# A hybrid two-layer decoder: mask building and two norms moved between engines, layer 1's rows kept in attention's order, and a planner with other costs

## The chip, the cores and the metric

One core of one Trainium2 chip runs the whole program: 1,024 tokens of width 1,024 through two layers, everything in float32. The engines are TensorE (PE; its weight loads are listed as PEld), VectorE (DVE), ScalarE (ACT), GpSimd (POOL) and SyncE (SP), which issues all DMAs. The metric is the device time of one execution in microseconds (us). The kernel before takes 2319.9 us, the median of three runs from 2319.55 to 2323.67.

## The reference

```python
for l in range(DEPTH):                       # DEPTH = 2
    h = rmsnorm(x, norm_mix_pre[l])
    if l % 2 == 0:
        proj = h @ w_in_even[e]              # 1024 -> 3072
        qa, fa, ia, ga, ub, vb = jnp.split(proj, splits, axis=-1)
        oa = hgrn2_mix(qa, fa, ia, ga, lb_all[l], a_norm[e])
        ob = chunk_gmlp_mix(gelu(ub), gelu(vb), b_ln_g[e], b_ln_b[e], b_ws[e], b_bias[e])
        mix = jnp.concatenate([oa, ob], axis=-1) @ w_out_even[e]
    else:
        mix = dilated_attention_mix(h, w_in_odd[o], positions) @ w_out_odd[o]
    x = x + rmsnorm(mix, norm_mix_post[l])
    h = rmsnorm(x, norm_ffn_pre[l])
    y = jnp.square(jax.nn.relu(h @ w_ff1[l])) @ w_ff2[l]      # 1024 -> 4096 -> 1024
    x = x + rmsnorm(y, norm_ffn_post[l])
```

`chunk_gmlp_mix` takes the layernorm of v over 512 channels, `(v - mu) * rstd * ln_g + ln_b`, and multiplies it in chunks of 128 positions by a causal 128x128 matrix per group of 128 channels, adds a bias per position and multiplies by u. `hgrn2_mix` ends in `rmsnorm(o, a_norm)` per head of 128 channels. The attention has three dilated branches, (128, 1), (512, 4) and (2048, 16), merged by their denominators: a key at distance d counts once, twice or three times, as it lies in one, two or three of them, so one additive mask with -inf, 0, ln 2 and ln 3 holds all three.

## The kernel before

Each float32 operand of a large product is split into a high part (ACT, a copy with rounding) and a low part (DVE or POOL, a subtraction), and each product is three matmuls (high x high, high x low, low x high). Six matmuls of 512 columns, listed as "x6", are one product of two 128-row blocks. `HT` and `WP` are the two large SBUF buffers of split activations and split weights; `b` stands for every other SBUF tile. The PSUM banks are `mm`, `tr`, `pa` and `pb`.

The program is first recorded, operation by operation, by the class `Plan` (`add`, line 257), and then put in order by `run` (line 344), which walks a planned time: at each step it takes an engine's ready operation, books it for its `cost` (line 297), and emits it. What it emits per engine is a list that the engine works off in order, each instruction waiting on semaphores for its inputs and for the release of its buffers. So an operation that has to wait holds up all behind it on its engine, and a cost in the planner changes the order and not the work. Large products are taken in the order of the program among those that are ready; the conversions are fitted in where the planner has an engine idle. A DVE operation that reads two SBUF tensors (`o["pair"]`, line 261) is booked longer while POOL is planned busy (line 459). In the profile nearly all instructions carry line 422, where `emit` issues them.

Stages, in order of time: constants (`consts0`, line 766, prepares the gMLP's transposed causal matrices `wsT` and its bias); layer 0's input projection with the HGRN and gMLP heads (`layer0_mix`, `gmlp_norm` 949, `gmlp_mix` 963, `onorm` 975), about 8 to 330 us; layer 0's output projection, then `ff1` and `ff2` (line 1572) to about 1068 us; attention, 1092 to about 1580; layer 1's output projection (it reads the attention's output back by `reload_oT`, line 1351), `ff1`, and `ff2` from about 2005 us to the end.

`ff2` runs three stages of eight blocks of hidden channels, each block eight products of six matmuls that go to eight PSUM banks, and at a stage's end DVE (and ACT) empty the banks into `y1` and `y2` (lines 1676 to 1685): `b<-tr,b`, `b<-pa,b` and the like in the rows. The first product of the next stage that goes to a bank waits for that. After them come the last products and, row tile by row tile, `post_part` and `post_end` (line 1761), which add the residual and store. Layers 0 and 1 run the same `ff2`; only in layer 0 it also builds the attention's mask: `attn_mask` (line 1093) makes a quarter of a 128x1024 table at each call, in one 128x1024 tile `x` (one buffer for all four calls), and stores it to DRAM (`maskd`).

```python
            if l == 0 and 3 <= m <= 6:                      # line 1687, m counts the blocks
                self.attn_mask(prep, 256 * (m - 3))
```

Each call is 4 iota and 15 further instructions on POOL and 2 on DVE (the two `bitwise_and`), which alternate on the same tile.

Attention works on the rows of a tile of 128 tokens in the order r, r+4, r+8, ... (four residues of 32). In the kernel before, `reload_oT` puts the columns of layer 1's activations back in token order while it splits them, with a strided source and target.

## Time and profile before

| what | us |
|---|---|
| median of three runs | 2319.9 |
| profiled execution | 2320.68 |
| its span, first to last instruction | 2318.9 |
| PE busy | 2259.9 (97% of the span) |
| DVE busy | 1616.1 (70%) |
| ACT busy | 1114.1 (48%) |
| POOL busy | 1097.3 (47%) |
| mean granted TensorE clock | 0.995 of full speed |

A row of the timeline reads: start, duration, engine, line, operation, output<-inputs, shape, count, and in brackets how long the engine was idle just before and who released it. "878.99 2.92 PE ... tr<-WP,HT ... x6 [7.30 <-DVE b L422]" is a product of six matmuls that began at 878.99 us and took 2.92, after PE had waited 7.30 us for a DVE instruction. Rows of the grouped view give count, busy time, mean ns of one, and the idle time before them. Rows of the windows view give start:end, length, and each engine's busy time in it.

### The profile page before, as it was taken

How to read it: one execution, taken by the hardware profiler on the slowest of the kernel's cores; microseconds unless marked ns; L12 is line 12 of the kernel's file. 1: busy time of each engine (PE TensorE's matmuls, PEld its weight loads, DVE VectorE, ACT ScalarE, POOL GpSimd, SP SyncE). 2: the span in 40 equal slices, each digit the busy share in tenths (PEclk: the TensorE clock that was granted, in tenths of full speed). 3: DMA queues.
4: the chain of work that ended last, by engine and by line, in shares of the span. 5: the costliest groups of instructions: out<-in, count | busy, mean ns of one | idle time of the engine just before them, and what ended most of it. 6: DMA issues, size and time to landing. Idle time of an engine off the chain costs nothing.

```text
span 2318.9 us, 32947 instructions
## 1 busy us (share of the span) xinstructions
PE 2259.9 (97%) x11314; PEld 1929.9 (83%) x11314; DVE 1616.1 (70%) x3106; ACT 1114.1 (48%) x2403; POOL 1097.3 (47%) x1184
## 2 busy tenths in 40 slices
PE   8999999999999998999999999998999999999998
PEld 7888778888888787887999999996788888888887
DVE  7688975665555955848888887877765555787746
ACT  6444444442222432435777777787452222433333
POOL 2121453355555889415555555543345555645204
PEclk9999999999999999999999999999999999999999
DMA  5110123334443957754311111114334443877654
GB/s 173 55 35 22 37 82 97 112 111 153 151 150 132 327 203 239 250 206 157 103 46 46 47 46 44 53 43 155 113 132 150 150 151 138 290 277 267 224 176 160
DMA packets 214768, 319.10 MB, mean 138 GB/s; under 512 B 14132, under 2 KB 99144, under 8 KB 214600
## 3 DMA queue, kind: packets, MB, share of 16 engines
q1 hardware_dynamic: 214600, 317.00, 40.5%
q8 instruction: 89, 1.46, 0.3%
q14 instruction: 79, 0.65, 0.1%
HBM read 226.24 MB, written 90.70 MB: 137 GB/s over the span
## 4 chain that ended last, share of the span: by engine, by line
PE 75%; DVE 12%; ACT 4%; POOL 3%; DMA 3%; issue 2%; SPq 0%; DVEq 0%; ACTq 0%; POOLq 0%
PE mm L422 34%; PE pa L422 20%; PE pb L422 13%; PE tr L422 9%; DVE b L422 9%; POOL b L422 3%; ACT b L422 3%; DVE WP L422 2%; DVE HT L422 1%; DMA b<-in_w_ff_dram 1%; DMA b<-in_w_in_odd_dram 1%; DMA b<-oTd 1%; DMA b<-hc 1%; ACT HT L422 0%; ACT WP L422 0%
## 5 line engine op out<-in xcount | busy, mean ns | idle before, releaser
L422 POOL TENSOR_TENSOR b<-b,b 128x512 f32<-128x512 f32 (+4 forms) x500 | 576.4, 1169 | 668.3 <-ACT b L422 324.5
L422 PE MATMUL mm<-WP,HT 128*128 128x512 f32 (+2 forms) x3744 | 822.5, 362 | 3.3 <-DVE HT L422 1.2
L422 PEld LDWEIGHTS mm<-WP,HT 128*128 128x128 f32 x3744 | 655.3, 190 | 82.1 <-DVE HT L422 2.3
L422 ACT ACTIVATE b<-b 128x512 f32<-128x512 f32 (+6 forms) x653 | 327.1, 513 | 369.8 <-POOL b L422 190.0
L422 POOL TENSOR_TENSOR b<-b 128x512 f32<-128x512 f32 (+4 forms) x368 | 331.8, 907 | 352.0 <-DVE b L422 246.0
L422 ACT ACTIVATE WP<-b 128x1024 fp32r<-128x1024 f32 (+2 forms) x248 | 194.3, 792 | 340.2 <-PE pb L422 190.5
L422 DVE TENSOR_TENSOR WP<-b,WP 128x1024 fp32r<-128x1024 f32 (+1 forms) x164 | 225.8, 1385 | 127.9 <-ACT WP L422 127.5
L422 DVE TENSOR_TENSOR b<-b,b 128x1024 fp32r<-128x1024 f32 (+6 forms) x382 | 239.3, 642 | 76.5 <-ACT b L422 58.7
L422 ACT ACTIVATE b<-mm 128x512 f32<-128x512 f32 (+3 forms) x346 | 152.6, 454 | 265.8 <-PE mm L422 246.2
L422 DVE TENSOR_TENSOR HT<-b,HT 128x1024 fp32r<-128x1024 f32 (+3 forms) x131 | 217.9, 1671 | 23.2 <-ACT HT L422 23.0
L422 PE MATMUL tr<-b,b 128*128 128x128 f32 x1074 | 171.1, 278 | 30.2 <-DVE b L422 24.2
L422 PE MATMUL pa<-WP,HT 128*128 128x512 f32 x768 | 193.8, 390 | 0.0
L422 DVE TENSOR_TENSOR b<-tr,b 64x128 fp32r<-64x128 f32 (+5 forms) x404 | 162.7, 407 | 32.8 <-ACT b L422 25.4
L422 PE MATMUL tr<-WP,HT 128*128 128x512 f32 x672 | 171.6, 392 | 7.6 <-DVE b L422 7.3
L422 ACT ACTIVATE HT<-b 128x1024 fp32r<-128x1024 f32 (+4 forms) x147 | 142.6, 973 | 73.8 <-PE mm L422 30.3
L422 PEld LDWEIGHTS tr<-b,b 128*128 128x128 f32 x1074 | 128.9, 147 | 54.1 <-DVE b L422 27.7
L422 PE MATMUL mm<-HT,b 128*128 128x512 f32 x720 | 173.7, 390 | 0.0
L422 PE MATMUL pa<-WP,b 128*128 128x512 f32 x720 | 173.6, 389 | 0.0
L422 DVE TENSOR_TENSOR b<-pa,b 128x512 f32<-128x512 f32 x110 | 75.4, 689 | 135.7 <-PE pa L422 135.6
L422 PEld LDWEIGHTS pa<-WP,HT 128*128 128x128 f32 x768 | 144.2, 188 | 29.9
L422 PEld LDWEIGHTS pa<-WP,b 128*128 128x128 f32 x720 | 134.9, 188 | 27.9
L422 PEld LDWEIGHTS mm<-HT,b 128*128 128x128 f32 x720 | 134.8, 188 | 27.8
(63 smaller groups left out, 3041.1 us busy)
## 6 DMA issues: line engine op xcount, KB each, us to landing
b<-in_w_ff_dram SPq DMA_DIRECT2D x172, 512.0 KB, 4.9
hc<-b SPq DMA_DIRECT2D x224, 256.0 KB, 2.1
b<-hc SPq DMA_DIRECT2D x112, 512.0 KB, 5.6
b<-in_w_in_odd_dram SPq DMA_DIRECT2D x64, 192.0 KB, 2.9
x<-b SPq DMA_DIRECT2D x24, 512.0 KB, 2.7
b<-x SPq DMA_DIRECT2D x24, 512.0 KB, 3.4
b<-in_w_in_even_dram SPq DMA_DIRECT2D x32, 256.0 KB, 2.8
wd<-b SPq DMA_DIRECT2D x16, 512.0 KB, 3.5
```

The source lines that it names most:

```text
L422: return getattr(self.real[eng], meth)(*[x.real() if isinstance(x, View) else x for x in a], **{k: x.real() if isinstance(x, View) else x ...
```

## The change

Five things change.

1. The planner's costs. A function `shares` says which DVE operations are booked longer beside POOL; POOL's costs rise (a 128x512 tensor_tensor from 147 + 2.15 x 512 to 150 + 2.4 x 512 ns); the longer booking itself gets another form.
2. The gMLP's layernorm no longer multiplies by `ln_g` and adds `ln_b` on POOL. The gain is applied after the causal product, as a column per channel group, by a DVE scalar_tensor_tensor of 128x128; the bias goes through the causal matrix once, in the constants (a product of ones with `wsT`, 2 float32 matmuls of 512 columns, and 8 scalar_tensor_tensors).
3. `onorm`: a DVE and a POOL tensor_tensor of 128x512 become four DVE scalar_tensor_tensors of 128x128.
4. `attn_mask`: all but the iota goes from POOL to DVE, and the calls stand at blocks 14, 16, 18 and 20 in place of 3 to 6.
5. Layer 1's rows stay in attention's order: `reload_oT` splits contiguously, its low part always on DVE; the residual rows of layer 1 are loaded, and the output rows stored, in four DMAs of 32 rows each.

```diff
-        o["pair"] = any(sum(isinstance(x, View) and x.buf.n not in self.inpsum and x.shape[-1] > 1
-                            for x in list(a)[1:] + [kw.get("in0"), kw.get("in1")]) > 1 for _, _, a, kw in calls)
+        o["pair"] = any(self.shares(*c) for c in calls)
...
-        return 147 + (2.15 if meth == "tensor_tensor" else 3.3 if meth == "tensor_scalar" else 1.2) * n
+        if meth == "memset":
+            return 62 + 0.83 * n
+        return 150 + (2.4 if meth == "tensor_tensor" else 4.0 if meth == "tensor_scalar" else 1.2) * n
+
+    def shares(self, eng, meth, a, kw):
+        views = [x for x in list(a) + [kw.get("in0"), kw.get("in1")] if isinstance(x, View) and x.shape[-1] > 0]
+        if any(x.buf.n in self.inpsum for x in views) or meth.startswith("dma"):
+            return False
+        out = kw["out"] if "out" in kw else a[0]
+        n = sum(x.shape[-1] > 1 or meth != "tensor_scalar" for x in views if x is not out)
+        return n > 1 or n == 1 and math.prod(out.shape[1:]) > 1
...
-                    end += min(max(free.get("POOL", 0.0) - at, 0.0), max(o["cost"], 700.0))
+                    busy = max(free.get("POOL", 0.0) - at, 0.0)
+                    if busy and now["POOL"]:
+                        busy += o["cost"]
+                    end += min(busy, max(0.85 * o["cost"], 700.0))
...
+                tr = self.tr_bank()
+                with nc.group():
+                    nc.tensor.matmul(tr, self.ones.bitcast(F32), wt.rearrange("p g t -> p (g t)"), start=True, stop=True)
+                for g in range(4):
+                    gs = slice(g * P, (g + 1) * P)
+                    nc.vector.scalar_tensor_tensor(bias[:, gs], tr[:, gs], lnb[:, g:g + 1], bias[:, gs], op0=OP.mult, op1=OP.add)
...
-        nc.gpsimd.tensor_tensor(vn, vn, self.lng, op=OP.mult)
-        nc.gpsimd.tensor_tensor(vn, vn, self.lnb, op=OP.add)
...
-        for i in range(2):
...
-            nc.vector.tensor_tensor(ob[t // 4][i][:, :, t % 4 * P:(t % 4 + 1) * P], part, bias, op=OP.add)
+        for g in range(4):
+            gs = slice(g * P, (g + 1) * P)
+            nc.vector.scalar_tensor_tensor(ob[t // 4][g // 2][:, g % 2, t % 4 * P:(t % 4 + 1) * P], tr[:, gs], self.lng[:, g:g + 1],
+                                           self.bias[t % 2][:, gs], op0=OP.mult, op1=OP.add)
...
-        nc.vector.tensor_tensor(ov, ov, r[:, :, None].to_broadcast([P, 4, P]), op=OP.mult)
-        nc.gpsimd.tensor_tensor(o, o, self.anr, op=OP.mult)
+        for h in range(4):
+            hs = slice(h * P, (h + 1) * P)
+            nc.vector.scalar_tensor_tensor(o[:, hs], o[:, hs], r[:, h:h + 1], self.anr[:, hs], op0=OP.mult, op1=OP.mult)
...
-            G.tensor_copy(u, d)
-            G.tensor_scalar(M, u, 128.0, None, op0=OP.is_le)
+            V.tensor_copy(u, d)
+            V.tensor_scalar(M, u, 128.0, None, op0=OP.is_le)
...
-        src = raw.rearrange("p k (r u) -> p k u r", r=4)
-        hi, lo = (self.HT[:, x, k0:k1, ts].rearrange("p k (u r) -> p k u r", r=4) for x in range(2))
-        nc.scalar.activation(hi, src, AF.Copy)
-        (nc.gpsimd if t < LAG["rel"] else nc.vector).tensor_tensor(lo, src, hi.bitcast(F32), op=OP.subtract)
+        hi, lo = (self.HT[:, x, k0:k1, ts] for x in range(2))
+        nc.scalar.activation(hi, raw, AF.Copy)
+        nc.vector.tensor_tensor(lo, raw, hi.bitcast(F32), op=OP.subtract)
+
+    def rows_of(self, x, t, cs, spread):
+        if not spread:
+            return [(slice(0, P), x[t * P:(t + 1) * P, cs])]
+        return [(slice(32 * r, 32 * r + 32), x[t * P + r:(t + 1) * P:4, cs]) for r in range(4)]
...
-            if l == 0 and 3 <= m <= 6:
-                self.attn_mask(prep, 256 * (m - 3))
+            if l == 0 and m in (14, 16, 18, 20):
+                self.attn_mask(prep, 128 * (m - 14))
...
-        nc.sync.dma_start(x, xin[rows, :])
+        for p, src in self.rows_of(xin, t, slice(0, D), xin is self.x2):
+            nc.sync.dma_start(x[p], src)
...
-                nc.sync.dma_start(xout[rows, d], x[:, d])
+                for p, dst in self.rows_of(xout, t, d, xout is self.out[0]):
+                    nc.sync.dma_start(dst, x[p, d])
```

How the instructions move. First DVE at the end of the first stage of layer 0's `ff2`. `b_6037` is the mask's tile before, `b_6054` after; `b<-tr` and `b<-pa` empty the banks. Before:

```order
L422 TENSOR_SCALAR b_6037<-b_6037 128x256
L422 TENSOR_TENSOR WP<-b_5958,WP 128x1024
L422 TENSOR_TENSOR WP<-b_6063,WP 128x1024
L422 TENSOR_SCALAR b_6037<-b_6037 128x256
L422 TENSOR_TENSOR b_6137<-tr,b_6137 128x512
L422 TENSOR_TENSOR HT<-b_6038,HT 128x2x512
L422 TENSOR_TENSOR b_6205<-tr,b_6205 128x512
L422 TENSOR_TENSOR HT<-b_5939,HT 128x2x512
L422 TENSOR_TENSOR b_5911<-pa,b_5911 128x512 x2
```

and after:

```order
L432 TENSOR_SCALAR b_6054<-b_6054 128x256
L432 TENSOR_TENSOR b_6054<-b_6054 128x256
L432 TENSOR_TENSOR WP<-b_6082,WP 128x1024
L432 TENSOR_TENSOR HT<-b_6105,HT 128x2x512
L432 TENSOR_TENSOR WP<-b_5963,WP 128x1024
L432 TENSOR_TENSOR b_6164<-tr,b_6164 128x512
L432 TENSOR_TENSOR HT<-b_5982,HT 128x2x512
L432 TENSOR_TENSOR b_6143<-tr,b_6143 128x512
L432 CAST b_6054<-b_6054 128x256
L432 TENSOR_SCALAR b_6054<-b_6054 128x256 x3
L432 TENSOR_TENSOR b_6054<-b_6054 128x256
L432 TENSOR_TENSOR b_5935<-pa,b_5935 128x512
```

Before, a mask instruction whose input comes from POOL stands directly ahead of the first emptying of a `tr` bank. After, three masks (54 instructions) are complete ahead of it, and the fourth begins between the `tr` and the `pa` banks, with a CAST whose input is POOL's iota.

Second PE at the end of layer 0, where the first transposes of layer 1's activations (`tr<-b_86`, 128x128) come between the last products of `ff2`. Before:

```order
L422 MATMUL tr<-WP,HT 128x512 x6
L422 MATMUL pa<-WP,HT 128x512 x3
L422 MATMUL tr<-b_86,b_6086 128x128 x4
L422 MATMUL pa<-WP,HT 128x512 x3
L422 MATMUL mm<-b_86,b_6086 128x128 x4
L422 MATMUL pb<-WP,HT 128x512 x6
```

and after:

```order
L432 MATMUL tr<-WP,HT 128x512 x6
L432 MATMUL pa<-WP,HT 128x512 x6
L432 MATMUL pb<-WP,HT 128x512 x6
L432 MATMUL tr<-b_86,b_6104 128x128 x4
L432 MATMUL pa<-WP,HT 128x512 x3
L432 MATMUL mm<-b_86,b_6104 128x128 x4
L432 MATMUL pa<-WP,HT 128x512 x3
```

The transposes stand one and a half products later. Third PE in layer 0's output projection, between two row tiles. Before:

```order
L422 MATMUL mm<-b_625,HT 128x512 x6
L422 MATMUL mm<-b_2727,HT 128x512 x6
L422 MATMUL mm<-WP,HT 128x512 x9
L422 MATMUL tr<-b_86,b_2611 128x128 x8
L422 MATMUL mm<-WP,HT 128x512 x27
```

and after:

```order
L432 MATMUL mm<-b_668,HT 128x512 x6
L432 MATMUL mm<-b_3001,HT 128x512 x6
L432 MATMUL mm<-WP,HT 128x512 x9
L432 MATMUL tr<-b_86,b_2358 128x128 x4
L432 MATMUL mm<-WP,HT 128x512 x6
L432 MATMUL tr<-b_86,b_2358 128x128 x4
L432 MATMUL mm<-WP,HT 128x512 x21
```

The eight transposes of a row tile are cut in two halves with one product between them.

## Rows read from the trace of the kernel before

**Rows 1.** The page's busy times, and from the view of waits who PE waited for (total us, times, longest).

```profile
PE 2259.9 (97%) x11314; PEld 1929.9 (83%) x11314; DVE 1616.1 (70%) x3106; ACT 1114.1 (48%) x2403; POOL 1097.3 (47%) x1184
...
PE tr L422 <- DVE b L422: 31.5, 20, 8.2
PE pa L422 <- DVE b L422: 6.5, 10, 1.9
PE tr L422 <- POOL b L422: 5.6, 6, 3.0
```

**Rows 2.** PE's timeline: the end of layer 0's `ff1` and the first stage of its `ff2` (to 878.99), where its last products begin (1054.62), and the same two places of `ff2` in layer 1 (2005.54 and 2266.78).

```profile
778.66 4.61 PE L422 MATMUL pa<-HT,b 128*128 128x512 f32 x12 [1.85 <-DVE b L422]
783.11 1.53 PE L422 MATMUL mm<-WP,HT 128*128 128x512 f32 x6
...
878.99 2.92 PE L422 MATMUL tr<-WP,HT 128*128 128x512 f32 x6 [7.30 <-DVE b L422]
...
1054.62 1.52 PE L422 MATMUL tr<-WP,HT 128*128 128x512 f32 x6
1055.98 1.52 PE L422 MATMUL pa<-WP,HT 128*128 128x512 f32 x6
...
2005.54 1.52 PE L422 MATMUL mm<-WP,HT 128*128 128x512 f32 x6
...
2266.78 1.52 PE L422 MATMUL tr<-WP,HT 128*128 128x512 f32 x6
```

**Rows 3.** Timeline of DVE and, in the second row, of POOL: two places in layer 0's `ff2` where a mask instruction of DVE stands.

```profile
775.54 2.47 DVE L422 TENSOR_SCALAR b<-b 128x256 int32<-128x256 int32 x1
775.27 2.59 POOL L422 TENSOR_TENSOR b<-b,b 128x1024 f32<-128x1024 f32 x1 [1.87 <-DMA b<-in_w_ff_dram]
...
866.75 0.29 DVE L422 TENSOR_SCALAR b<-b 128x256 int32<-128x256 int32 x1 [12.31 <-POOL b L422]
...
878.04 0.29 DVE L422 TENSOR_SCALAR b<-b 128x256 int32<-128x256 int32 x1 [6.32 <-POOL b L422]
878.25 0.68 DVE L422 TENSOR_TENSOR b<-tr,b 128x512 f32<-128x512 f32 x1
```

**Rows 4.** Windows: the first stage of `ff2` in layer 0, the 16.5 us ahead of layer 1's, and layer 1's first stage. Columns: start:end, length, busy us of PE, PEld, DVE, ACT, POOL with counts, granted clock, DMA share, GB/s.

```profile
783.10:870.10 87.00, 87.00 (x385) 72.05 (x384) 62.61 (x38) 33.99 (x36) 80.26 (x53) 1.00 0.70 246
...
1989.00:2005.50 16.50, 16.50 (x74) 13.69 (x73) 12.23 (x12) 8.25 (x11) 5.82 (x3) 1.00 0.85 295
2005.50:2092.50 87.00, 87.00 (x385) 71.84 (x385) 75.66 (x42) 36.87 (x40) 50.28 (x18) 1.00 0.84 296
```

**Rows 5.** Groups by form on DVE: the mask's integer tensor_scalars in 783 to 957 us (count, busy us, mean ns, idle before), and all tensor_tensors of 128x256 of SBUF tiles in the program.

```profile
L422 DVE TENSOR_SCALAR b<-b 128x256 int32<-128x256 int32 x7 | 2.0, 292 | 45.5 <-POOL b L422 45.5
...
L422 DVE TENSOR_TENSOR b<-b,b 128x256 f32<-128x256 f32 x64 | 31.4, 490 | 1.8 <-PE pa L422 1.5
```

**Rows 6.** The heads of layer 0, 230 to 330 us: PE's wait for POOL, and groups by form on POOL and DVE (the last row are scalar_tensor_tensors of 128x128).

```profile
PE tr L422 <- POOL b L422: 4.9, 5, 3.0
...
L422 POOL TENSOR_TENSOR b<-b,b 128x512 f32<-128x512 f32 x33 | 45.2, 1375 | 71.7 <-DVE b L422 67.2 <-ACT WP L422 2.7 <-PE tr L422 1.3
...
L422 DVE TENSOR_TENSOR b<-tr,b 128x256 f32<-128x256 f32 x16 | 6.0, 413 | 0.0
L422 DVE TENSOR_TENSOR b<-b,b 128x512 f32<-128x512 f32 x8 | 5.4, 679 | 0.0
...
L422 DVE SCALAR_TENSOR_TENSOR b<-b,b,tr 128x128 f32<-128x128 f32 x3 | 1.0, 344 | 0.1
```

**Rows 7.** PE's timeline at the transposes in layer 0's output projection (the first and the last of three such rows) and at the first transposes of layer 1's activations.

```profile
398.78 0.66 PE L422 MATMUL tr<-b,b 128*128 128x128 f32 x4 [0.75 <-DVE b L422]
...
424.30 0.66 PE L422 MATMUL tr<-b,b 128*128 128x128 f32 x4 [0.75 <-DVE b L422]
...
1065.63 0.66 PE L422 MATMUL tr<-b,b 128*128 128x128 f32 x4 [3.37 <-DVE b L422]
```

**Rows 8.** The end of attention: a window of it, then groups by form of the whole program: the splits of `reload_oT` (`HT<-b,HT` 128x512) beside contiguous splits of the same size.

```profile
1564.00:1582.00 18.00, 13.32 (x66) 8.73 (x65) 17.37 (x49) 17.19 (x34) 11.45 (x18) 1.00 0.39 128
...
L422 DVE TENSOR_TENSOR HT<-b,HT 128x512 fp32r<-128x512 f32 x13 | 17.0, 1308 | 4.9 <-ACT HT L422 4.7
L422 DVE TENSOR_TENSOR b<-b,b 128x512 fp32r<-128x512 f32 x42 | 29.8, 709 | 2.6 <-ACT b L422 2.4
```

**Rows 9.** The end of the program on SP's queue (a load, then six stores of half a row tile) and on DVE, and two lines of the list of DMA issues (KB each, median us from issue to landing).

```profile
2297.05 0.33 SPq L422 DMA_DIRECT2D b<-x  x1
2298.47 17.28 SPq L422 DMA_DIRECT2D out_dram<-b  x6
2313.98 1.41 DVE L422 SCALAR_TENSOR_TENSOR b<-b,b,b 128x512 f32<-128x512 f32 x2
...
out_dram<-b SPq DMA_DIRECT2D x16, 256.0 KB, 2.1
...
vd<-b SPq DMA_DIRECT2D x32, 64.0 KB, 1.5
```

**Rows 10.** PE's timeline in the constants: float32 matmuls of 128 columns (each is two records) and what follows them.

```profile
90.80 0.71 PE L422 MATMUL pa<-b,b 128*128 128x128 f32 x4
91.27 0.95 PE L422 MATMUL mm<-HT,WP 128*128 128x512 f32 x3
```

**Rows 11.** Window over attention.

```profile
1092.00:1556.00 464.00, 458.49 (x2829) 434.57 (x2828) 372.56 (x1144) 350.40 (x1020) 231.93 (x582) 1.00 0.17 53
```

More of the change, by code (lines that the diff above doesn't have):

```diff
@@ L805, in consts0 @@
                     nc.vector.tensor_scalar(self.masks[:, l, q * P:(q + 1) * P], xf, float(1 << l), None, op0=OP.is_lt)
+            self.lng, lnb = pool.tile([P, 4], F32, name="lng"), pool.tile([P, 4], F32, name="lnb")
+            for x, src in ((self.lng, a["b_ln_g"]), (lnb, a["b_ln_b"])):
+                nc.sync.dma_start(x, bass.AP(tensor=src.tensor, offset=src.offset, ap=[[1, P], [P, 4]]))
             ge = tp.tile([P, P], F32, name="ge")
@@ L970, in gmlp_mix @@
                                  start=True, stop=True)
-        for i in range(2):
-            part, bias = (x[:, 256 * i:256 * i + 256].rearrange("p (g t) -> p g t", g=2) for x in (tr, self.bias[t % 2]))
-            nc.vector.tensor_tensor(ob[t // 4][i][:, :, t % 4 * P:(t % 4 + 1) * P], part, bias, op=OP.add)
+        for g in range(4):
+            gs = slice(g * P, (g + 1) * P)
+            nc.vector.scalar_tensor_tensor(ob[t // 4][g // 2][:, g % 2, t % 4 * P:(t % 4 + 1) * P], tr[:, gs], self.lng[:, g:g + 1],
+                                           self.bias[t % 2][:, gs], op0=OP.mult, op1=OP.add)
     def onorm(self, pool, o):
@@ L1103, in attn_mask @@
                 G.iota(d[32 * r:32 * r + 32], pattern=[[-1, n]], base=S - P - c0 + r, channel_multiplier=4)
-            G.tensor_copy(u, d)
-            G.tensor_scalar(M, u, 128.0, None, op0=OP.is_le)
-            self.nc.vector.tensor_scalar(e, d, 3, None, op0=OP.bitwise_and)
-            G.tensor_scalar(t, e, 0, None, op0=OP.is_equal)
-            G.tensor_tensor(M, M, t, op=OP.add)
-            G.tensor_scalar(t, u, 512.0, None, op0=OP.is_le)
-            G.tensor_tensor(M, M, t, op=OP.add)
-            G.tensor_scalar(M, M, -1.0, 0.0, op0=OP.add, op1=OP.max)
-            self.nc.vector.tensor_scalar(e, d, 15, None, op0=OP.bitwise_and)
-            G.tensor_scalar(t, e, 0, None, op0=OP.is_equal)
-            G.tensor_tensor(M, M, t, op=OP.add)
-            G.tensor_scalar(t, u, 0.0, None, op0=OP.is_ge)
-            G.tensor_tensor(M, M, t, op=OP.mult)
-            G.tensor_scalar(t, M, 0.0, NEG, op0=OP.is_equal, op1=OP.mult)
-            G.tensor_scalar(u, M, 2.0, LN2_8, op0=OP.is_equal, op1=OP.mult)
-            G.tensor_tensor(t, t, u, op=OP.add)
-            G.tensor_scalar(u, M, 3.0, LN3_8, op0=OP.is_equal, op1=OP.mult)
-            G.tensor_tensor(t, t, u, op=OP.add)
+            V.tensor_copy(u, d)
+            V.tensor_scalar(M, u, 128.0, None, op0=OP.is_le)
+            V.tensor_scalar(e, d, 3, None, op0=OP.bitwise_and)
+            V.tensor_scalar(t, e, 0, None, op0=OP.is_equal)
+            V.tensor_tensor(M, M, t, op=OP.add)
+            V.tensor_scalar(t, u, 512.0, None, op0=OP.is_le)
+            V.tensor_tensor(M, M, t, op=OP.add)
+            V.tensor_scalar(M, M, -1.0, 0.0, op0=OP.add, op1=OP.max)
+            V.tensor_scalar(e, d, 15, None, op0=OP.bitwise_and)
+            V.tensor_scalar(t, e, 0, None, op0=OP.is_equal)
+            V.tensor_tensor(M, M, t, op=OP.add)
+            V.tensor_scalar(t, u, 0.0, None, op0=OP.is_ge)
+            V.tensor_tensor(M, M, t, op=OP.mult)
+            V.tensor_scalar(t, M, 0.0, NEG, op0=OP.is_equal, op1=OP.mult)
+            V.tensor_scalar(u, M, 2.0, LN2_8, op0=OP.is_equal, op1=OP.mult)
+            V.tensor_tensor(t, t, u, op=OP.add)
+            V.tensor_scalar(u, M, 3.0, LN3_8, op0=OP.is_equal, op1=OP.mult)
+            V.tensor_tensor(t, t, u, op=OP.add)
             self.nc.sync.dma_start(self.maskd[:, c0:c0 + n], t)
@@ L1763, in post_end @@
         nc = self.nc
-        rows = slice(t * P, (t + 1) * P)
         x = pl.tile([P, D], F32, name="x", tag="gpre" if last else "x")
-        nc.sync.dma_start(x, xin[rows, :])
+        for p, src in self.rows_of(xin, t, slice(0, D), xin is self.x2):
+            nc.sync.dma_start(x[p], src)
         r = self.rstd_act(ss)
```

5 lines of the change are left out of this document (1 added, 4 removed).

## The prediction

> **What bounds the kernel now.** I read the page first: PE is busy for 2259.9 us of the span of 2318.9, and nothing else is near that [rows 1]. So the time changes only where PE waits, where its clock falls, or at the two ends. The view of PE's waits came next: by far the most is waited for DVE at the `tr` bank, then at `pa`, and 5.6 us for POOL [rows 1]. PE's timeline tells where these waits lie, and the windows and the groups by form tell what keeps DVE and POOL there.
>
> The largest lies in layer 0's `ff2`. Layer 1 runs the same stages without a mask and serves as a measure: from the first product to the first of the last products layer 0 takes 1054.62 - 783.11 = 271.5 us, layer 1 2266.78 - 2005.54 = 261.2 [rows 2]. The difference of 10.3 us has its main place at the first stage's end: PE waits 7.30 us for a `tr` bank, and the product behind the wait takes 2.92 us instead of 1.52, as at the lower of the clock's two levels, 1.2 in place of 2.4 GHz [rows 2]. Ahead of that bank's emptying DVE holds a mask instruction that itself waits: 12.31 us at 866.75 and again 6.32 at 878.04, both times for POOL, and the emptying follows at 878.25 [rows 3]. POOL is busy for 80.3 of that stage's 87 us [rows 4], and DVE stood idle for 45.5 us in front of seven such mask instructions [rows 5].
>
> **The change part by part.** All sums are against the profiled execution, 2320.7 us, which is 0.8 above the median.
>
> A, the mask on DVE. The waits of DVE for POOL's half of the mask go. At most layer 0 becomes like layer 1, 10.3 us, plus what the same kind of instruction costs at 775.54, where it took 2.47 us [rows 3] and PE's next 12 matmuls came 1.85 us late and took 4.61; at full speed six start 1.36 us after the last six (1054.62 to 1055.98) and drain for 0.16 more, so twelve take 2.88, and the loss was 1.85 + 1.73 = 3.6 [rows 2]. The most is thus 13.9. What is late next is DVE itself. The order puts three whole masks, 54 instructions, ahead of the first emptying. One mask is 12 at 0.292 us and 6 at 0.49 [rows 5], 6.4 us; three are 19.3. Layer 1's first stage leaves DVE 87.0 - 75.7 = 11.3 us, and the 16.5 us ahead of it another 4.3 [rows 4]; DVE comes 19.3 - 15.6 = 3.7 us late. A bank is missed only when the product ahead of its next use, 1.4 us, is through, so PE waits about 2.3 [rows 2]. A = -13.9 + 2.3 = -11.5; its ends are -13.9 and, with the stall kept, -2.3 (first rival).
>
> B, the two norms. POOL loses 24 tensor_tensors of 128x512. PE waited 4.9 us for POOL there, and POOL's 33 such instructions took 45.2 us, 1.38 each [rows 6], so 33 us of POOL's work go. DVE loses 16 at 0.413 and 8 at 0.679, 12.0 us, and gets 64 scalar_tensor_tensors of 128x128 at 0.344, 22.0 [rows 6]; ten more, on an engine that has little room here. Against that stands that DVE meets POOL less often, beside which an instruction can take long, as at 775.54 [rows 3]. I take a third of the wait back, -1.5. Ends: all of POOL's wait gone, -5, or 3 of the ten us shown on PE, +3.
>
> C, the cut transposes in layer 0's output projection. Three times PE waits 0.75 us for DVE [rows 7]; the second half now stands a product of 1.36 us later, which covers that. -2.0, between -2.25 and 0.
>
> D, the first transposes of layer 1's activations: PE waits 3.37 us for DVE's norm [rows 7]. They move back by one and a half products, 2.0 us. -2.0, between -3.4 and 0.
>
> E, layer 1's rows. The strided splits took DVE 13 x 1.308 = 17.0 us, contiguous ones 0.709 each, 7.8 us less [rows 8]; ACT's high parts lose their stride too. Only what PE waits counts: in 1564 to 1582 it is busy for 13.3 of 18 us with DVE and ACT both above 17 [rows 8]. The splits are a part of DVE's load, so I take half of that 4.7 us, -2.5; the ends are 0 and -8, the whole of DVE's saving. The low parts that come from POOL to DVE cost it little at 0.7. The loads of the residual rows, four DMAs in place of one, lie on SP far ahead of their use, and the last row's is issued before the last stores; nothing.
>
> F, the last stores. SP issues six stores from 2298.47 to 2315.75, and DVE's last instruction ends at 2315.39 [rows 9]. The last two half tiles become 2 x 4 DMAs; SP needs 0.33 us for one (the load at 2297.05) [rows 9]. The first half is ready when the first of DVE's last two instructions is through, about 2314.7; eight issues from there end at 2317.3, 1.6 us later than now. Landing is 2.1 us for 256 KB and 1.5 for 64 KB [rows 9], which could give 0.6 back. +1.6, between +1.0 and +2.0.
>
> G, the bias in the constants: 2 float32 matmuls of 512 columns. Two of 128 columns took 0.47 us, from 90.80 to 91.27 [rows 10]; 0.235 each, 0.94 for 512 columns, 1.9 for two. They come where PE has few other things ready, but I count them in full: +1.9, from 0. The eight small DVE instructions behind them, 2.8 us at 0.344, come long before the first use of the bias.
>
> The planner's new costs change no work. In the large products PE's order is the same in both; what they change is the order on DVE and POOL, and it is counted in A, C and D, apart from attention (second rival).
>
> Sum: -11.5 - 1.5 - 2.0 - 2.0 - 2.5 + 1.6 + 1.9 = -16.0, so 2304.7 for the profiled execution and 2303.9 on the median's scale: 2304.
>
> **The rivals.** First, the stall stays with another cause. The fourth mask's CAST stands on DVE between the `tr` and the `pa` banks, waits for POOL's iota, and its tile is the one buffer whose last contents SP must first have stored; behind it stand the `pa` emptyings and the next splits. For it speaks that DVE waited 6 and 12 us for POOL at just this place [rows 3]; against it that POOL is relieved of all the other mask work, and so is not 80 us busy but nearer to layer 1's 50 [rows 4]. With a stall of 8 and the clock's 3.6 still there, A is -13.9 + 11.6 = -2.3, and the time 2304 + 9.2 = 2313.
>
> Second, the order in attention turns out worse. PE is busy for 458.5 of 464 us there [rows 11], so there is little to win; 64 groups of products, each with its own chain through DVE, ACT and POOL, got a new order from the planner's costs. At 0.2 us a group PE loses 13 us: 2317, no change that could be told. For it speaks only that DVE is 372.6 us busy there and so often in use [rows 11]; against it that the waits are now so few that the order must be poor for such a loss.
>
> Third, on the side of slower: each mask instruction on DVE is held by POOL. At 775.54 one took 2.47 us, and ended at 778.01, as POOL's tensor_tensor that began at 775.27 ended at 777.86 [rows 3]; the seven others took 0.29 [rows 5], but these had POOL waiting or just beginning. POOL is busy for 50.3 us of layer 1's first stage [rows 4], and DVE's 42 instructions there pay for part of that already, as 75.7 / 42 = 1.80 us each shows. Half of POOL's time, 25 us, could fall on the 54 mask instructions; DVE would then be 3.7 + 25 = 28.7 us late and PE wait 27.3. The other terms give -4.5; a stall that ends above 13.9 + 4.5 = 18.4 us makes the kernel slower, that is DVE 19.8 late, from (19.8 - 3.7) / 54 = 0.30 us more per mask instruction on. At the full 25 us: 2319.9 - 4.5 - 13.9 + 27.3 = 2329.
>
> The Trainium skill has the rule for this (SBUF — State Buffer, section "SBUF: two separate sides"): VectorE, in a two-port mode or with two inputs from SBUF, and GpSimd lock one pair of ports for a whole instruction, and whoever comes later is blocked until the other has ended. The instruction at 775.54 ends with POOL's and agrees; by the rule alone all mask instructions that meet POOL are held and the time would be the 2329, by the seven at 0.29 us it is the sum above.
>
> Fourth, more goes than I count: A in full (2.3), D's whole wait (1.4) and E's whole 8 (5.5): 2304 - 2.3 - 1.4 - 5.5 = 2295.
>
> **How the numbers follow.** My forecast has 0.68, the first rival 0.10, the second 0.09, the third 0.08, the fourth 0.05. About 0.2% (4.6 us) is what a measurement of this kernel tells from no change: faster ends at 2315.3, slower begins at 2324.5. Forecast, first (but for 0.01) and fourth are faster: 0.68 + 0.09 + 0.05 = 0.82. No change holds the second and the 0.01: 0.10. Slower is the third, 0.08. The range of 8 in 10 goes from 2294 to 2316, which leaves out the second and the third and little of the fourth; the likeliest case has 2298 to 2311.
>
> **What the new profile would show.** For A: no stall of over 3 us at `tr` in the first stage, layer 0's 271.5 us at 262 to 264, DVE's mask instructions at 0.3 to 0.5 us in the mean and DVE without waits for POOL. For B: PE's wait for POOL before 330 us under 3 us. For C and D: the waits of 0.75 gone, and 1.4 or so left of the 3.37. For E: splits of `reload_oT` at 0.7 on DVE and 0.6 on ACT, and less than 4.7 us idle in the 18 us. For F: SP's last issue some 1.6 us behind DVE's last instruction plus what it is now. I am wrong if mask instructions take over 0.6 us in the mean, if a new wait of several us shows in attention, or if PE is short of splits in layer 0's second stage.

## The result, and the profile after

The changed kernel takes 2292.86 us, the median of four runs from 2288.75 to 2296.32; before stands at 2319.78 beside it. The ratio is 0.9879 with a 95% interval of 0.9858 to 0.9901. I had forecast 2304 with 2294 to 2316: the direction was right, the gain is 27 us where I had 16, and the time lies just below the range. The profiled execution took 2294.83 us.

The page's busy times and PE's waits of the changed kernel, as in [rows 1]:

```profile
PE 2250.0 (98%) x11318; PEld 1927.4 (84%) x11318; DVE 1634.5 (71%) x3218; ACT 1109.4 (48%) x2403; POOL 976.5 (43%) x1096
...
PE tr L432 <- DVE b L432: 18.4, 9, 8.6
PE pa L432 <- DVE b L432: 3.5, 6, 1.2
...
PE tr L432 <- POOL b L432: 0.5, 1, 0.5
```

PE is busy 10 us less with the same products, and waits for DVE at `tr` 18.4 us instead of 31.5. Of these, 8.2 and 8.6 us are one wait, for the first data at the start. The wait for POOL, 5.6 us, has shrunk to 0.5.

To see where the time went I took the starts of the same matmuls in both traces (each 512-column matmul counted from the first, without the bias products of the constants) and compared the stretches between them. The numbers are us more or less than in before; "own" is the length in before.

| stretch | own | forecast | changed kernel | once more | planner only | norms only | mask only | rows only |
|---|---|---|---|---|---|---|---|---|
| start, to the first 512-column matmul | 69.3 | +1.9 (G) | +3.4 | +3.5 | +1.1 | +4.1 | +0.4 | +0.9 |
| heads of layer 0 | 263.6 | -1.5 (B) | -9.1 | -9.2 | -8.2 | -8.0 | 0.0 | 0.0 |
| layer 0's output projection | 106.2 | -2.0 (C) | -2.5 | -2.8 | -2.5 | +1.0 | 0.0 | +0.1 |
| `ff1` | 336.7 | 0 | 0.0 | 0.0 | -0.1 | -0.2 | -0.2 | +0.2 |
| `ff2` of layer 0 | 286.1 | -11.5 (A) | -8.5 | -8.2 | -6.5 | -0.3 | -10.0 | -0.5 |
| to layer 1's first products | 43.9 | -2.0 (D) | -3.9 | -3.8 | -3.7 | 0.0 | -0.1 | -0.1 |
| attention | 401.3 | 0 | -6.4 | -6.5 | -6.3 | +0.9 | +0.1 | -0.4 |
| its end and the projection | 176.9 | -2.5 (E) | -2.2 | -4.5 | +1.6 | -0.1 | -0.2 | -5.0 |
| layer 1's feed-forward | 626.7 | 0 | +0.2 | +0.2 | +0.1 | +0.5 | +0.6 | -0.1 |
| from the last matmul's start to the end | 8.2 | +1.6 (F) | +2.9 | +3.0 | 0.0 | -0.1 | +0.1 | +2.5 |
| span | 2318.9 | -16.0 | -26.2 | -28.3 | -24.6 | -2.4 | -9.3 | -2.5 |

A second execution of the changed kernel (the column "once more") repeats all but one stretch within 0.4 us; that one, the end of attention, moves by 2.3. Another kernel below (`best`), profiled twice, repeats within 0.3 us but for `ff2`, which moves by 1.7. So `ff2` and the end of attention can be read to about 2 us, the other stretches to half a microsecond. The single-part columns are the experiments below.

`ff2`'s first stage in layer 0, as in [rows 4]: the stretch ahead, the stage, and the next one. Then DVE's groups by form in the stage, the mask's own.

```profile
754.70:771.20 16.50, 16.50 (x75) 13.65 (x74) 10.93 (x10) 8.81 (x10) 9.01 (x9) 1.00 0.75 258
771.20:858.20 87.00, 87.00 (x385) 72.06 (x384) 86.00 (x90) 37.68 (x39) 45.56 (x24) 1.00 0.78 274
858.20:945.20 87.00, 83.31 (x360) 68.48 (x359) 74.55 (x61) 31.92 (x32) 39.95 (x19) 0.98 0.80 284
```

```profile
L432 DVE TENSOR_TENSOR b<-b 128x256 f32<-128x256 f32 x17 | 9.4, 550 | 0.5
L432 DVE TENSOR_SCALAR b<-b 128x256 f32<-128x256 f32 x20 | 7.8, 401 | 0.4
...
L432 DVE TENSOR_SCALAR b<-b 128x256 f32<-128x256 int32 x6 | 3.9, 653 | 0.1
L432 DVE TENSOR_SCALAR b<-b 128x256 int32<-128x256 int32 x6 | 3.9, 648 | 0.0
L432 DVE CAST b<-b 128x256 f32<-128x256 int32 x3 | 3.0, 1015 | 0.0
```

DVE is now full, 86.0 of 87 us, where POOL was before. The 52 mask instructions in the stage take 9.4 + 7.8 + 3.9 + 3.9 + 3.0 = 28.0 us, 0.54 each, not the 0.36 that I took. So DVE comes late, and PE's timeline shows it:

```profile
863.44 2.08 PE L432 MATMUL tr<-WP,HT 128*128 128x512 f32 x6 [3.69 <-DVE b L432]
865.32 2.73 PE L432 MATMUL mm<-WP,HT 128*128 128x512 f32 x6
```

PE waits 3.69 us and then works below full speed for two products (granted clock 0.63 from 863.4 to 868.0 us). The wait is half of the 7.30 in [rows 2], and it is the mechanism I named for what would be left, with 2.3 us.

In the heads (the window and PE's waits are those of [rows 6], 230 to 330 us) no wait of PE for POOL is left, and POOL is busy for 18.0 of 100 us. The second fence has, from 225 to 325 us, what POOL still does of this size and then the new instructions of the two norms: `onorm`'s, then those of `gmlp_mix`.

```profile
230.00:330.00 100.00, 99.87 (x488) 83.97 (x487) 87.22 (x346) 48.22 (x139) 18.03 (x15) 1.00 0.21 64
```

```profile
L432 POOL TENSOR_TENSOR b<-b,b 128x512 f32<-128x512 f32 x9 | 12.8, 1425 | 93.6 <-DVE b L432 93.5
...
L432 DVE SCALAR_TENSOR_TENSOR b<-b,b,b 128x128 f32<-128x128 f32 x32 | 11.5, 408 | 0.0
L432 DVE SCALAR_TENSOR_TENSOR b<-tr,b,b 128x128 f32<-128x128 f32 x32 | 9.0, 343 | 3.2 <-PE tr L432 3.2
```

PE's timeline at the places of [rows 7]: the two halves of a row tile's transposes, the first of layer 1, and a later pair of it.

```profile
392.01 0.60 PE L432 MATMUL tr<-b,b 128*128 128x128 f32 x4
...
393.84 0.60 PE L432 MATMUL tr<-b,b 128*128 128x128 f32 x4
...
1047.45 0.60 PE L432 MATMUL tr<-b,b 128*128 128x128 f32 x4
...
1060.81 0.66 PE L432 MATMUL tr<-b,b 128*128 128x128 f32 x4 [1.61 <-DVE b L432]
```

No wait is left at the first two or at the first transposes of layer 1 (3.37 before). A later transpose waits 1.61.

Attention, in windows that begin and end with the same matmuls, first before, then after:

```profile
1105.80:1507.10 401.30, 396.24 (x2457) 376.44 (x2456) 323.18 (x998) 306.55 (x895) 208.10 (x521) 1.00 0.18 54
```

```profile
1085.20:1480.00 394.80, 390.65 (x2458) 375.54 (x2457) 324.80 (x995) 306.28 (x890) 205.69 (x521) 1.00 0.18 55
```

The stretch is 6.5 us shorter with the same matmuls, and 5.6 of that lie in PE's *busy* time, 396.2 against 390.7. That is why I did not see it: in [rows 11] only 5.5 us of 464 looked idle.

The end, as in [rows 9]:

```profile
2279.16 11.14 SPq L432 DMA_DIRECT2D out_dram<-b  x24
...
2285.10 1.41 DVE L432 SCALAR_TENSOR_TENSOR b<-b,b,b 128x512 f32<-128x512 f32 x2
...
out_dram<-b SPq DMA_DIRECT2D x64, 64.0 KB, 1.7
```

### The profile page after: what moved, and what is told of

It is laid out like the page before. It is cut to its first block, busy times and chain, and to the rows that moved or that the text cites. A ratio compares the mean times of both kernels' runs of the same rounds, so it can differ in the third digit from the quotient of the medians.

```text
span 2292.7 us, 33047 instructions
## 1 busy us (share of the span) xinstructions
PE 2250.0 (98%) x11318; PEld 1927.4 (84%) x11318; DVE 1634.5 (71%) x3218; ACT 1109.4 (48%) x2403; POOL 976.5 (43%) x1096
## 4 chain that ended last, share of the span: by engine, by line
PE 82%; DVE 7%; DMA 4%; issue 2%; ACT 2%; POOL 2%; SPq 1%; DVEq 0%; POOLq 0%; ACTq 0%
PE mm L432 41%; PE pa L432 20%; PE pb L432 12%; PE tr L432 10%; DVE b L432 4%; ACT b L432 2%; DVE HT L432 2%; POOL b L432 1%; DVE WP L432 1%; DMA b<-hc 1%; DMA b<-oTd 1%; SPq L432 1%; DMA b<-in_w_in_even_dram 0%; DMA b<-in_x_dram 0%; DMA b<-x 0%
## 5 line engine op out<-in xcount | busy, mean ns | idle before, releaser
L432 POOL TENSOR_TENSOR b<-b,b 128x512 f32<-128x512 f32 (+4 forms) x477 | 538.1, 1145 | 749.1 <-ACT b L432 320.8
L432 POOL TENSOR_TENSOR b<-b 128x512 f32<-128x512 f32 (+4 forms) x343 | 303.3, 892 | 360.4 <-DVE b L432 292.4
L432 ACT ACTIVATE b<-mm 128x512 f32<-128x512 f32 (+3 forms) x346 | 153.2, 455 | 282.6 <-PE mm L432 266.7
L432 DVE TENSOR_TENSOR b<-b,b 128x1024 fp32r<-128x1024 f32 (+6 forms) x351 | 223.8, 656 | 71.0 <-ACT b L432 61.5
L432 DVE TENSOR_TENSOR HT<-b,HT 128x1024 fp32r<-128x1024 f32 (+3 forms) x131 | 203.9, 1562 | 19.2 <-ACT HT L432 18.9
L432 DVE TENSOR_TENSOR b<-tr,b 64x128 fp32r<-64x128 f32 (+4 forms) x388 | 157.0, 407 | 42.3 <-ACT b L432 35.3
L432 ACT ACTIVATE HT<-b 128x1024 fp32r<-128x1024 f32 (+4 forms) x147 | 134.5, 916 | 75.1 <-DMA b<-hc 38.8
L432 ACT ACTIVATE b<-tr 64x128 fp32r<-64x128 f32 (+3 forms) x376 | 134.6, 360 | 53.7 <-PE tr L432 45.0
```

Source lines behind the costliest of these rows:

```text
L432: return getattr(self.real[eng], meth)(*[x.real() if isinstance(x, View) else x for x in a], **{k: x.real() if isinstance(x, View) else x ...
```

## The experiments

**One part at a time.** My theory after the result: the planner's costs bring most of what I missed, by another order, not by less work. The rival: it comes from the work taken off POOL. The kernel before got one part of the change alone. The planner's (`p_only`):

```diff
+        o["pair"] = any(self.shares(*c) for c in calls)
...
-        return 147 + (2.15 if meth == "tensor_tensor" else 3.3 if meth == "tensor_scalar" else 1.2) * n
+        return 150 + (2.4 if meth == "tensor_tensor" else 4.0 if meth == "tensor_scalar" else 1.2) * n
...
-                    end += min(max(free.get("POOL", 0.0) - at, 0.0), max(o["cost"], 700.0))
+                    end += min(busy, max(0.85 * o["cost"], 700.0))
```

> Only the planner's new costs (part 1 of the change) on the kernel before; nothing else. Theory 1 (the gain I missed comes from the order): 2308 us, about -12: attention (first to last of its products) 6 us shorter as in the changed kernel, the waits of 0.75 in layer 0's output projection gone (-2.5), the first transposes of layer 1 -2, some 2 to 3 in the heads. Theory 2 (it comes from the work taken off GpSimd, the order gives only what I counted in C and D): 2315, about -4.5, attention unchanged.

Measured: 2297.27 us, ratio 0.9905 [0.989, 0.992]; the span is 24.6 us shorter, of 26.2 in the whole change. The theory holds, though its number, -12, was only half of what came. The mask still is POOL's work in this kernel, and yet 6.5 us of `ff2` are gone. Its DVE timeline shows how (compare [rows 3]); the last row is PE's:

```profile
852.59 0.68 DVE L432 TENSOR_TENSOR b<-tr,b 128x512 f32<-128x512 f32 x1
...
855.94 0.68 DVE L432 TENSOR_TENSOR b<-tr,b 128x512 f32<-128x512 f32 x1
...
871.13 0.29 DVE L432 TENSOR_SCALAR b<-b 128x256 int32<-128x256 int32 x1 [12.44 <-POOL b L432]
871.34 0.68 DVE L432 TENSOR_TENSOR b<-pa,b 128x512 f32<-128x512 f32 x1
...
872.08 2.54 PE L432 MATMUL pa<-WP,HT 128*128 128x512 f32 x6 [1.95 <-DVE b L432]
```

A mask instruction of DVE still waits 12.44 us for POOL. But it stands behind the emptying of the two `tr` banks and of one `pa`, ahead of one `pa` alone, and PE waits 1.95 us for that where it had waited 7.30. The wait was not removed; it was moved past what PE needs.

The norms (`n_only`), the mask (`m_only`) and the rows (`r_only`), each alone:

```diff
-        nc.gpsimd.tensor_tensor(vn, vn, self.lng, op=OP.mult)
-        nc.gpsimd.tensor_tensor(vn, vn, self.lnb, op=OP.add)
...
-            G.tensor_copy(u, d)
+            V.tensor_copy(u, d)
...
-        hi, lo = (self.HT[:, x, k0:k1, ts].rearrange("p k (u r) -> p k u r", r=4) for x in range(2))
+        hi, lo = (self.HT[:, x, k0:k1, ts] for x in range(2))
```

> Only the two norms (parts 2 and 3) on the kernel before, with the old costs of the planner. Theory 1: the heads (70 to 333 us) gain at most 3 us and the constants cost 3: no change, 2320. Theory 2: the heads gain the 9 us that the changed kernel shows there, less 3 at the start: 2314.

Measured: 2317.84, ratio 0.9992 [0.9983, 1.0001]. The heads are 8.0 us shorter, as the rival said, the start is 4.1 longer, and the run as a whole is not told from before. Planner and norms each take the heads' waits for POOL away, and together they bring 9.1, not 16.

> Only the mask (part 4) on the kernel before, old costs. Theory 1 and 2 alike: the stall at the end of ff2's first stage in layer 0 shrinks from 7.3 us to under 4 and the loss of 3.6 before it goes, about -12, 2308. Rival: without the new costs, which book DVE's instructions longer beside GpSimd, the mask's 54 instructions stand worse and the stall stays: -4, 2316.

Measured: 2311.75, ratio 0.997 [0.9959, 0.9981]; `ff2` 10.0 us shorter. That is my A but for 1.5 us. The time lies midway between the two cases, but the rival, that the mask needs the new costs, would have given only 4 us, and `ff2` alone gives 10.0, so it falls.

> Only layer 1's rows (part 5) on the kernel before, old costs. By my terms E and F: -2.5 + 1.6, 2319; with the tail as the changed kernel shows it (2.9 longer): 2320, no change. Rival: the contiguous splits shorten the end of attention and the start of the projection by 5 us or more: 2317.

Measured: 2318.73, ratio 0.9995 [0.9986, 1.0005]: 5.0 us less at the end of attention and 2.5 more at the end of the program. The two expectations were each right for one half.

**One part left out.** The changed kernel with the mask as before (`no_m`), with the norms as before (`no_n`), with the rows as before (`no_r`); the edits are the reverse of those above.

> The changed kernel with the mask built as before (on GpSimd, at blocks 3 to 6); all else changed. If the parts add: the mask's 7.5 us are lost, 2300.5. If the planner's costs and the mask remove the same stall twice: 2295 to 2297, with a stall of 5 us or more left in layer 0's ff2.

> The changed kernel with the two norms as before. If the new costs and the norms remove the same waits for GpSimd in the heads: the heads lose 2 us, the start wins 2.7 back, 2292. If they add: 2295 or more.

> The changed kernel with layer 1's rows as before. The end is 2.8 us shorter (7.9 instead of 10.7), the end of attention and the projection 4 us longer as in the run of the planner's costs alone: 2294. If the rows bring nothing beside the new costs: 2290.

Measured: 2297.31, 2290.66 and 2295.89 us. Beside the planner's costs the mask is worth 5.7 us of `ff2` (-2.8 without it, -8.5 with it), less than its 10.0 alone: the two meet at the same stall. By the stretches the norms cost more than they bring: without them the start is 3.1 us shorter and the heads 1.1 longer; the medians, 2290.66 and 2292.86, don't tell the two apart. The rows bring 2.8 us at the end of attention (5.1 by the second execution) and cost 2.8 at the end. The ratios, 0.9902 [0.9887, 0.9917] without them and 0.9879 [0.9858, 0.9901] with them, don't show that they bring anything beside the other parts.

**Which of the planner's costs.** POOL's durations alone (`p_pool`), and the two rules on DVE alone (`p_dve`), on the kernel before.

> Of the planner's new costs only GpSimd's durations (the return line of cost), on the kernel before. Theory a (the old durations had GpSimd ready too early, so PE's list put instructions ahead of results that were not there): the heads 7 us shorter, the stall in layer 0's ff2 smaller by 5 or more, in all -12 or more, 2307. Theory b (what matters is how DVE is booked beside GpSimd): -5, 2314, attention unchanged.

> Of the planner's new costs only the two on DVE (the function shares and the new form of the longer booking), GpSimd's durations as before. Theory a: -6, 2313 (attention's order and the cut transposes), the heads unchanged. Theory b: -15 or more, 2304, heads and attention as with all new costs.

Measured: 2307.88 and 2309.9 us, ratios 0.9945 [0.9929, 0.9961] and 0.9953 [0.9936, 0.9971]. Neither theory alone: each gives about half. `p_pool` meets the time of theory a, but the heads gave it 2.9 us and not 7. `ff2` comes from POOL's durations (-7.4 against +2.1), the heads from both (-2.9 and -5.2), and attention's 6.3 us in full only from the two together (+0.7 and -3.5).

**Nearer, and farther, durations.** POOL's durations in the changed kernel 2% and 10 to 22% higher (`cost_near`, `cost_hi`), and in the kernel before lower still (`cost_lo`):

```diff
-        return 150 + (2.4 if meth == "tensor_tensor" else 4.0 if meth == "tensor_scalar" else 1.2) * n
+        return 150 + (2.45 if meth == "tensor_tensor" else 4.08 if meth == "tensor_scalar" else 1.2) * n
...
+        return 150 + (2.65 if meth == "tensor_tensor" else 4.9 if meth == "tensor_scalar" else 1.2) * n
...
-        return 147 + (2.15 if meth == "tensor_tensor" else 3.3 if meth == "tensor_scalar" else 1.2) * n
+        return 147 + (1.9 if meth == "tensor_tensor" else 2.6 if meth == "tensor_scalar" else 1.2) * n
```

> The changed kernel with GpSimd's durations 2% off (2.45 and 4.08 in place of 2.4 and 4.0). If the gain rests on durations that are about right: within 2 us of 2292.9. If small shifts throw the order about: 4 us or more away, either side.

> The changed kernel with GpSimd's planned durations higher still (150 + 2.65 n for tensor_tensor and 150 + 4.9 n for tensor_scalar, near what the trace of before shows beside DVE: 2.8 us for 128x1024). If nearness to the measured durations is what helps: 2290 or less. If the order only happened to fall well: anywhere in 2285 to 2310, and not where nearness would put it.

> The kernel before with GpSimd's planned durations shorter still (147 + 1.9 n for tensor_tensor, 147 + 2.6 n for tensor_scalar); nothing else. If durations that are too short are what makes PE wait: slower than before, 2325 or more. If the order before was only an unlucky one, and any other is better: 2318 or less.

Measured: 2295.83, 2294.36 and 2317.35 us; the ratio of `cost_lo` is 0.9994 [0.9985, 1.0003]. The gain stands when the durations rise. Beyond that the times decide nothing: `cost_near` is 3 us off, between its two cases; `cost_hi` is not better than the changed kernel, where nearness to the measured durations wanted 2290 or less; and `cost_lo` is not slower, as the theory wanted, but lies where the rival put it, that the order before was an unlucky one.

The stretches tell more (one execution each, us against before; the waits are PE's own, for POOL in the heads and for DVE at the end of `ff2`'s first stage):

| kernel | POOL's durations | rules on DVE | heads | wait for POOL there | `ff2` | wait at the stage's end | attention |
|---|---|---|---|---|---|---|---|
| `cost_lo` | lower | old | +1.1 | 7.4 | +3.4 | 9.19 | -3.8 |
| before | old | old | 0 | 4.9 | 0 | 7.30 | 0 |
| `p_pool` | new | old | -2.9 | 4.1 | -7.4 | none | +0.7 |
| `p_dve` | old | new | -5.2 | 2.5 | +2.1 | 10.17 | -3.5 |
| `p_only` | new | new | -8.2 | 0.7 | -6.5 | 1.95 | -6.3 |

```profile
PE tr L422 <- POOL b L422: 7.4, 5, 4.0
PE tr L433 <- POOL b L433: 4.1, 4, 2.6
PE tr L430 <- POOL b L430: 2.5, 3, 1.7
PE tr L432 <- POOL b L432: 0.7, 3, 0.3
...
880.07 2.93 PE L422 MATMUL tr<-WP,HT 128*128 128x512 f32 x6 [9.19 <-DVE b L422]
1065.76 1.11 PE L422 MATMUL tr<-b,b 128*128 128x128 f32 x4 [3.76 <-DVE b L422]
...
870.81 2.93 PE L430 MATMUL tr<-WP,HT 128*128 128x512 f32 x6 [10.17 <-DVE b L430]
```

The first four lines are the heads of `cost_lo`, `p_pool`, `p_dve` and `p_only`, the next two `cost_lo`, the last `p_dve`. Under the same rules on DVE, longer durations for POOL shorten the heads, the wait for POOL in them, and the wait at the stage's end, each time. (`ff2` as a whole is 3.4 us longer in `cost_lo` because the first transposes, with 3.76 us of wait, fall into that stretch there; the way to layer 1 is 6.0 shorter for it.) The new durations are also nearer to the trace: 128x512 took 1.375 us [rows 6], the old formula gives 1.25 and the new one 1.38. That an order planned with longer durations for POOL removes PE's waits is thus shown for the heads and `ff2`. Whether it is the nearness that counts is not: with the highest ones, of `cost_hi`, the heads (-10.0) and `ff2` (-14.0) gain still more.

For attention no such order shows, and its gain hangs on how the order happens to fall: 2% more in `cost_near` leaves 1.5 of its 6.4 us, and `cost_lo` has 3.8 of them with no other change. Why one order is better there stays open.

**The end.** All rows of a half tile in one DMA (`one_dma`), and the last row tile's stores from two queues (`two_queues`):

```diff
-        return [(slice(32 * r, 32 * r + 32), x[t * P + r:(t + 1) * P:4, cs]) for r in range(4)]
+        return [(slice(0, P), x[t * P:(t + 1) * P, cs].rearrange("(u r) d -> r u d", r=4))]
...
-                    nc.sync.dma_start(dst, x[p, d])
+                    (nc.scalar if last and p.start in (32, 96) else nc.sync).dma_start(dst, x[p, d])
```

> The changed kernel, but each half row of the output, and each residual row tile of layer 1, goes in one DMA whose DRAM side has three levels (residue, row, column) in place of four DMAs of 32 rows. If the 2.9 us that the end grew by are SP's issues: the stretch from PE's end to the last instruction falls from 10.7 to about 8 us, 2290.5. Rival (the order of rows in DRAM costs it in the transfer itself): it stays at 10 or more, 2293.

> The changed kernel with the last row tile's eight stores issued from two queues, half from ACT's and half from SP's. If SP's eight issues in a row made the end 2.9 us longer: the stretch from PE's end to the last instruction falls from 10.7 to about 9 us, 2291. If the four-way stores land later by themselves: it stays at 10.7.

Measured: 2324.7 us, slower than before by a ratio of 1.0014 [1.0005, 1.0024], and 2295.78. In `one_dma` SP's issues are few and soon done, and the end is 29 us behind PE's last matmul. (Another 7 us are lost at the end of attention and in the projection, with one wait of PE of 7.70 us; the residual rows are loaded in the same form there.) Timeline of DVE and SP, and the window behind the last issues:

```profile
2298.57 1.41 DVE L432 SCALAR_TENSOR_TENSOR b<-b,b,b 128x512 f32<-128x512 f32 x2 [5.85 <-DMA b<-x]
...
2295.58 9.42 SPq L432 DMA_DIRECT2D out_dram<-b  x6
...
2304.00:2317.00 13.00, 0.00 (x0) 0.00 (x0) 0.21 (x1) 0.00 (x0) 0.00 (x0) 0.50 0.22 84
```

The last store is issued by 2305.0 and the program ends at 2317.4; DVE waits 5.85 us for a residual row that must wait for the stores ahead of it. The DMA engines' mean share is 0.22 in that window, 3.5 of 16 engines, though nothing else is left to do. So this form is slow in the transfer itself, and the run does not tell what SP's issues cost. The share fits a rule of the Trainium skill (DMA: Bandwidth & Descriptors, section "Rules for kernel authors"): a DMA runs on no more engines than its outermost dimension has elements, here four. A window's mean cannot show which engines they were, but 3.5 lies under that four. `two_queues` was no gain either, but it is no test of two free queues: ACT issued its four stores at once, while SP stood still from 2283.7 to 2286.7, 2.9 us of it waiting for a store to land, and its last eight then came one behind the other until 2290.3.

So the backlog itself was tested: stores of whole rows, four for a row tile instead of eight, except for the last row tile (`wide_out`).

```diff
-            if xout is self.out[0] or c.start:
-                d = slice(c.start if xout is self.out[0] else 0, c.stop)
+            if last or c.start:
+                d = slice(c.start if last else 0, c.stop)
```

> The changed kernel, but layer 1's output rows are stored in four DMAs of 32 x 1024 instead of eight of 32 x 512, except those of the last row tile. If SP's backlog of stores of the tiles before is what makes the end longer: PE's end to the last instruction falls from 10.7 to 9 us or less, 2291. If it is the last tile's eight alone: 10.7 stays.

Measured: the end is 1.6 us longer than before, not 2.9, so nearly half of the cost was the backlog of stores of the tiles ahead. The time, 2293.4 us, does not tell it from the changed kernel.

**A version that beats both.** The changed kernel without the norms' change and with the wider stores (`best`), and again side by side with the changed kernel (`best_again`, `all_again`).

> The changed kernel without the two norms' change and with the wider stores: 2290.7 for the norms left as before, less what the wider stores bring (1.7): 2289. If the two don't add: 2290.7.

> The changed kernel once more, unaltered, on the same chip as the next one, to set the two side by side and to see how far one execution's profile repeats: 2292 to 2295; PE's wait in layer 0's ff2 3 to 4 us as before.

> The changed kernel without the norms' change and with the wider stores, once more: 2285 to 2287, so that it beats the changed kernel by 6 us or more. If the 7 us between the two medians came from the chip they ran on: less than 4.

Measured: 2285.55, then 2286.57 against 2293.47 on the same chip; ratio to before 0.985 [0.9835, 0.9864], beside 0.9886 [0.9869, 0.9902] for the changed kernel. The start is 3.8 us shorter than in the changed kernel, `ff2` 3 to 5, the end 1.3; the heads are 1 us longer. In `best` PE has one wait of 1.6 us in `ff2`:

```profile
PE pa L432 <- DVE b L432: 1.6, 1, 1.6
```

That `ff2` gains too was not asked for. It is measured, in two executions, and not explained.

## Why the prediction was wrong

**The sum.** Forecast -16.0, measured -26.2 on the spans. Too small were B by 7.6, attention by 6.4, D by 1.9, C by 0.5; too large A by 3.0; the costs G and F were higher by 1.5 and 1.3. That the time came so near to the range is in part luck, since these errors have both signs. (Two of the forecast's terms are rounded against each other: -13.9 + 2.3 is -11.6, and half of 4.7 is 2.35; the sum stands.) The failing step is the paragraph on the planner: "The planner's new costs change no work", and what they change "is counted in A, C and D, apart from attention". It is true that no work changes; but alone these costs bring 24.6 us, where C and D were to give 4.0 and A only together with the mask's move.

**B** was right in what it named, POOL's lateness, and wrong in size. I took a third of 4.9 us back. Both the planner alone and the norms alone removed nearly all of it, and more than the waits list. From start to start, against the median of neighbours of the same kinds, the matmuls from 235 to 333 us had lost 5.7 us in gaps above 0.35 and 2.4 in gaps of 0.1 to 0.35; after it is 0 and 0.3. With the norms DVE did not become the bound; it is busy for 87.2 of 100 us in that window, and of the new instructions 32 took 0.408 us and 32 the 0.343 that I had reckoned with.

**Attention** I put at nothing because PE looked busy for 458.5 of 464 us [rows 11], and gave my second rival, that the order there turns worse, 0.09. The order turned better. Where PE waits a tenth or two between matmuls, the profile shows it as busy: counted from start to start in the same way, the stretch of 401.3 us had lost 5.5 us in gaps of 0.1 to 0.35 and 5.7 in longer ones, after 1.2 and 5.2. So there was something to win; that this order would win it nothing in the rows told, and 2% on the durations takes most of it back. The right reading would have been the time per matmul, compared with a stretch of the same instructions without waits.

**A** was right in mechanism and in what is late next. Two things in it were off. The stall did not need the mask's move: moving the waiting instruction past the `tr` banks was enough, and the planner did that alone. And a mask instruction took 0.54 us and not 0.36, which left a wait of 3.69 us instead of 2.3; with the two slow products behind it (2.08 and 2.73 us for 1.52 each), which I counted for before but not for what would be left, the rest of the stall costs 5.5 us. That is the 3 us by which A was too large. From the first product to the first of the last ones layer 0 takes 266.7 us, not the 262 to 264 of the forecast. My first rival, that the fourth mask's CAST would hold the `pa` banks, did not come: the only wait in that stage is at `tr`.

**The third rival** was partly there, and far from deciding: 0.18 us more per mask instruction, where it would have needed 0.30. The timeline has the lock that I had read from one row at 775.54, twice in a row here, POOL's rows and DVE's, and a split of DVE's beside a quiet POOL:

```profile
848.93 3.17 POOL L432 TENSOR_TENSOR b<-b,b 128x1024 f32<-128x1024 f32 x1 [3.62 <-DMA b<-in_w_ff_dram]
...
855.91 2.40 POOL L432 TENSOR_TENSOR b<-b,b 128x1024 f32<-128x1024 f32 x1 [3.81 <-DMA b<-in_w_ff_dram]
...
849.75 3.43 DVE L432 TENSOR_TENSOR WP<-b,WP 128x1024 fp32r<-128x1024 f32 x1
...
856.00 2.59 DVE L432 TENSOR_TENSOR b<-b 128x256 f32<-128x256 f32 x1
...
860.44 1.22 DVE L432 TENSOR_TENSOR HT<-b,HT 128x1024 fp32r<-128x1024 f32 x1
```

POOL ends at 852.10 and at 858.31; DVE's instructions that began meanwhile end at 853.18 and 858.59, 1.08 and 0.28 later. A split of this size takes 1.22 when POOL is quiet. So DVE did not share, it stood until POOL was through. The Trainium skill says the same (SBUF — State Buffer, section "SBUF: two separate sides"): an exclusive lock, held for the whole instruction. What the rule does not give is how often it hits; here the mean of 0.54 us says it, beside a POOL that is busy for 45.6 of 87 us.

**The fourth rival**, that more goes than I count, put the time at 2295, near to what came, but by other terms: of its three only D went whole, A fell short of the sum, and E gave 2.2 and 4.5, not 8. My three signs of being wrong did not come at all: a mask instruction stayed under 0.6 us in the mean, attention had no new wait of several us, and PE was not short of splits.

**C** came as forecast, and **D** with 3.9 for 2.0. The whole wait of 3.37 went, where I had left 1.4 of it, and with it the slow products behind it, which I had not counted (before, the granted clock was 0.61 from 1065.6 to 1070.0 us). The later wait of 1.61 stands against that. **E** came with 2.2 and 4.5 in two executions of the change, 5.0 alone; the splits fell to 0.743 us on DVE as expected. **F** was mis-sized in two steps: SP takes 11.14 / 24 = 0.46 us per store, not 0.33, and the tiles ahead still had stores in the queue when the last tile was done. DVE's last instruction ends at 2286.5, and the last store is issued by 2290.3, 3.8 us later; before it was 0.4 [rows 9]. **G**: the two matmuls are 4 records with 2.0 us in all, as forecast; the start still lost 3.4, and what the rest is stays open.

## What to carry to other kernels

Where an order is planned, the durations in the plan are part of the kernel: a consumer put ahead of its input stalls its whole engine, and here a few numbers and one rule were worth more (24.6 us alone) than all moved work (2.4, 9.3 and 2.5, each alone). Judge "busy" by the time per instruction against a stretch that has no waits, not by the share. Price a part beside the others, since two remedies for one stall bring it back once.
